# Gate, up and down projections by seven half-size products each, with activations and residual kept in DRAM

## The chip, the cores and the metric

The kernel runs on one core of a Trainium2 chip. The metric is the device time of one execution in microseconds (us). The engines are TensorE (PE in the profile), VectorE (DVE), ScalarE (ACT), GpSimd (POOL) and SyncE (SP), which issues most DMAs. Each engine works through its own instructions in a fixed order and waits on semaphores where an instruction needs another engine's or a DMA's result.

## The reference

One decoder block on x of shape (1, 1024, 1024) in float32. 16 meta tokens stand ahead of the 1024 tokens, and their outputs are dropped. The feed-forward width is 2816.

```python
def mixer(xn, w_in, conv_a_w, conv_b_w, ..., w_out):
    b_gate, c_gate, h_a, glu_val, glu_gate = jnp.split(einsum("btd,de->bte", xn, w_in), ...)
    y_a = b_gate * causal_depthwise_conv(c_gate * h_a, conv_a_w)          # 3 taps
    g = glu_val * sigmoid(glu_gate)
    y_b = silu(layer_norm(causal_depthwise_conv(g, conv_b_w) + conv_b_bias))  # 31 taps
    return einsum("bte,ed->btd", concatenate([y_a, y_b], -1), w_out)

def swiglu(xn, w_gate, w_up, w_down):
    return einsum("btf,fd->btd", silu(xn @ w_gate) * (xn @ w_up), w_down)

h = concatenate([meta_tokens, x])
h = h + rms_norm(mixer(rms_norm(h, pre_mix_norm), ...), post_mix_norm)
h = h + rms_norm(swiglu(rms_norm(h, pre_ffn_norm), ...), post_ffn_norm)
return h[:, 16:]
```

## The kernel before, in words

Every float32 product is made of three products in the fast format: an operand is split into a high part (a cast on ACT) and a low part (value minus high part, by a subtraction on DVE or GpSimd), and `mm3` (lines 87 to 90) issues high × high, high × low and low × high into one PSUM bank. A weight "unit" of 128x1024 is loaded by SP (`load_unit`, L74) and split (`split_unit`, cast L80, subtraction L81).

The stages, in the order in which PE works through them:

1. Input projection with both convolution groups, to about 270 us. The change leaves it as it is, apart from the size of the tiles that hold x.
2. Output projection in three groups of 128-token tiles, (0,1,2), (3,4,5) and (6,7) (L439 to L454): the banks are called po. `leave_psum` squares and scales what they hold, `post_mix` (L410 to L415) makes the root of the norm (`rsqrt_n`, L93 to L111, 8 or 9 operations of 128x1 on DVE) and the residual h, and `ffn_norm` (L417 to L433) normalises h (hn), transposes it on PE (pt, 8 transposes a tile) and splits it into hT. Here only tiles 0 to 3 are normalised.
3. Feed-forward, one half of the tokens (512) at a time (L458). Gate and up: for each of 22 blocks of 128 columns, 2 × 8 × 3 matmuls of 128x512 into the two banks pf (L460 to L466); then SiLU on ACT (L470) and the product on DVE (L471) leave ga, and all 22 of these tiles stay in SBUF.
4. Down, for each half of the output columns (L478): 22 blocks × 4 token tiles × 3 matmuls into four banks pd. ga is split again into gs (L492, L493). During the first of these stages `ffn_norm` of tiles 4 to 7 is run (L499 to L502). After each stage the four banks are squared (jo, L511) and scaled (L514); after the second one the root is made, the residual is added (L520 to L523) and the tile stored (L524).

So each weight of gate, up and down is loaded and split twice, once for each half of the tokens, and the residual h of all tiles stays in SBUF. The tile framework derives the order of the instructions on each engine from the program with a scheduler; tiles come from rotating pools, and an instruction that writes a tile waits until the tile's last user is done.

## Time and profile before

| | |
|---|---|
| time, median of 3 runs | 1118.02 us (1117.54 to 1118.24) |
| span of the profiled execution | 1117.3 us |
| PE, DVE, ACT, POOL busy | 1078.5, 621.2, 384.9, 217.6 us |
| first gate/up matmul | 371.05 us |
| last down matmul | 1107.25 us |
| bytes moved | 107.38 MB |

A row of the costliest groups reads: source line, engine, operation, output tile <- input tiles, shapes, number of instructions | busy time, mean ns of one | idle time of the engine just before them and what ended it. A row of the timeline begins with the start and the duration in us, and ends with the idle time before it in brackets. A row of the windows gives the stretch, its length, busy time and number of instructions (of the engine or tile chosen, otherwise of PE, PEld, DVE, ACT and POOL in this order), the granted clock, the DMA share and GB/s. PEld is the loading of a matmul's stationary operand. Matmuls overlap, so the distance between starts is their cost, not the duration.

### The profile page before, as it was taken

What the parts mean: (1) busy time and instruction counts of PE and PEld (TensorE: products, weight loads), DVE (VectorE), ACT (ScalarE), POOL (GpSimd) and SP (SyncE); (2) the same over time, 40 slices, a digit from 0 to 9 for tenths busy, and PEclk for the clock granted to TensorE, in tenths of its full rate; (3) what the DMA queues carried; (4) which work ended last, traced back from release to release, by engine and by line L of the source; (5) the groups of instructions that cost most, each with busy time, mean ns of one, the idle gap of its engine ahead of it and who ended that gap; (6) DMA issues with size and microseconds to landing.
All of it is one profiled execution on the core that took longest, in us unless ns stands there. A gap on an engine that the chain in (4) does not pass through costs nothing.

```text
span 1117.3 us, 12633 instructions
## 1 busy us (share of the span) xinstructions
PE 1078.5 (97%) x5039; PEld 909.7 (81%) x5039; DVE 621.2 (56%) x890; ACT 384.9 (34%) x508; POOL 217.6 (19%) x104
## 2 busy tenths in 40 slices
PE   8999979897998999999999999999999999999996
PEld 8999978796876888888888887888888888888885
DVE  6499999999489843322222555474333222244545
ACT  7345221236544522222222444343222222233432
POOL 3579755254555100000000000010000000000001
PEclk9999989898999999999999999999999999999999
DMA  7111111112463432223223232234222223322222
GB/s 269 57 39 57 38 38 38 39 39 94 143 234 132 132 95 94 94 95 94 94 95 96 92 95 94 94 119 145 94 95 94 95 94 97 97 92 93 97 73 75
DMA packets 30874, 107.38 MB, mean 96 GB/s; under 512 B 3424, under 2 KB 3808, under 8 KB 30816
## 3 DMA queue, kind: packets, MB, share of 16 engines
q1 hardware_dynamic: 30240, 104.94, 28.6%
q10 hardware_dynamic: 576, 1.65, 0.5%
q8 instruction: 39, 0.64, 0.2%
q14 instruction: 19, 0.16, 0.0%
HBM read 102.38 MB, written 4.19 MB: 95 GB/s over the span
## 4 chain that ended last, share of the span: by engine, by line
PE 77%; DVE 18%; ACT 1%; issue 1%; DMA 1%; SPq 0%; DVEq 0%
PE pf L89 15%; PE pf L88 15%; PE pf L90 14%; PE pd L88 7%; PE pd L90 7%; PE pd L89 7%; DVE acc L272 6%; DVE z L272 5%; PE po L89 1%; PE po L90 1%; PE po L88 1%; PE p_in_g L88 1%; PE p_in_v L88 1%; PE p_in_v L89 1%; PE p_in_g L89 1%
## 5 line engine op out<-in xcount | busy, mean ns | idle before, releaser
L521 POOL TENSOR_TENSOR raw<-raw,h 128x512 f32<-128x512 f32 x6 | 8.4, 1392 | 734.3 <-ACT raw L520 734.3
L81 DVE TENSOR_TENSOR wl_u<-ws_u,wh_u 128x1024 fp32r<-128x1024 f32 x44 | 53.9, 1225 | 164.1 <-ACT wh_u L80 164.0
L89 PE MATMUL pd<-wl_d,gs 128*128 128x512 f32 x352 | 138.9, 395 | 0.0
L90 PE MATMUL pd<-wh_d,gs 128*128 128x512 f32 x352 | 138.0, 395 | 0.0
L89 PE MATMUL pf<-hT,wh_g 128*128 128x512 f32 x352 | 138.0, 392 | 0.0
L89 PE MATMUL pf<-hT,wh_u 128*128 128x512 f32 x352 | 138.0, 392 | 0.0
L88 PE MATMUL pf<-hT,wh_g 128*128 128x512 f32 x352 | 137.9, 392 | 0.0
L88 PE MATMUL pf<-hT,wh_u 128*128 128x512 f32 x352 | 137.9, 392 | 0.0
L88 PE MATMUL pd<-wh_d,gs 128*128 128x512 f32 x352 | 137.6, 396 | 0.0
L90 PE MATMUL pf<-hT,wl_g 128*128 128x512 f32 x352 | 137.5, 391 | 0.0
L90 PE MATMUL pf<-hT,wl_u 128*128 128x512 f32 x352 | 137.5, 391 | 0.0
L471 DVE TENSOR_TENSOR ga<-pf,ga 128x512 f32<-128x512 f32 x44 | 30.4, 692 | 145.0 <-PE pf L90 145.0
L493 DVE TENSOR_TENSOR gs<-ga,gs 128x512 fp32r<-128x512 f32 x88 | 60.4, 690 | 86.8 <-ACT gs L492 76.5
L80 ACT CAST wh_u<-ws_u 128x1024 fp32r<-128x1024 f32 x44 | 46.2, 1050 | 178.6 <-PE pf L89 169.7
L272 DVE SCALAR_TENSOR_TENSOR acc<-g,pr,acc 128x512 f32<-128x512 f32 x146 | 99.8, 746 | 0.0
L80 ACT CAST wh_g<-ws_g 128x1024 fp32r<-128x1024 f32 x44 | 46.2, 1050 | 152.8 <-PE pf L89 104.4
L492 ACT CAST gs<-ga 128x512 fp32r<-128x512 f32 x88 | 54.3, 620 | 114.5 <-PE pd L89 112.4
L88 PEld LDWEIGHTS pd<-wh_d,gs 128*128 128x128 f32 x352 | 66.2, 188 | 15.9 <-ACT gs L492 0.3
L90 PEld LDWEIGHTS pd<-wh_d,gs 128*128 128x128 f32 x352 | 66.2, 188 | 15.8
L89 PEld LDWEIGHTS pd<-wl_d,gs 128*128 128x128 f32 x352 | 66.2, 188 | 15.5
L90 PEld LDWEIGHTS pf<-hT,wl_u 128*128 128x128 f32 x352 | 66.1, 188 | 14.9
L90 PEld LDWEIGHTS pf<-hT,wl_g 128*128 128x128 f32 x352 | 66.1, 188 | 15.0
(201 smaller groups left out, 2116.6 us busy)
## 6 DMA issues: line engine op xcount, KB each, us to landing
ws_g<-w_gate_u SPq DMA_DIRECT2D x44, 512.0 KB, 3.4
ws_u<-w_up_u SPq DMA_DIRECT2D x44, 512.0 KB, 3.4
ws_d<-w_down_u SPq DMA_DIRECT2D x44, 512.0 KB, 3.4
ws_o<-w_out_u SPq DMA_DIRECT2D x24, 512.0 KB, 3.4
xs<-xT SPq DMA_DIRECT2D x8, 520.0 KB, 7.3
h<-x_tok SPq DMA_DIRECT2D x8, 512.0 KB, 8.1
out<-raw SPq DMA_DIRECT2D x16, 256.0 KB, 2.0
ws_in_c<-w_in_u SPq DMA_DIRECT2D x4, 512.0 KB, 3.4
```

The costliest lines, as they stand in the source:

```text
L80: nc.scalar.copy(wh, ws)
L81: (eng or nc.gpsimd).tensor_tensor(wl, ws, wh.bitcast(F32), op=ALU.subtract)
L88: nc.tensor.matmul(o, lh, rh, start=start, stop=False)
L89: nc.tensor.matmul(o, lh, rl, start=False, stop=False)
L90: nc.tensor.matmul(o, ll, rh, start=False, stop=stop)
L272: nc.vector.scalar_tensor_tensor(o if j == CB - 1 else p, s, wb(a, j), o if j == HEAD[a] else p, op0=ALU.mult, op1=ALU.add)
L471: nc.vector.tensor_tensor(g, p[1], g, op=ALU.mult)
L492: nc.scalar.copy(s[:, 0, :], gt[f])
L493: nc.vector.tensor_tensor(s[:, 1, :], gt[f], s[:, 0, :].bitcast(F32), op=ALU.subtract)
L521: nc.gpsimd.tensor_tensor(y, y, ht[ti][:, dq], op=ALU.add)
```

## The change

One level of Strassen's scheme (Winograd's form) is put on the three matrices. A matrix is cut into 2 × 2 blocks, and seven products of half-size operands take the place of eight; sums of blocks are formed before and after.

- **Tokens.** All eight tiles are normalised before the feed-forward. The transposed tokens are kept as four raw blocks (half of the channels × half of the tokens), from which the seven token operands X are made once: B11, B21, B22 and the sums T1 to T4 (`split_big`, `halves`). `ffn_norm` writes B11 directly.
- **Gate and up.** Class `Pair` does two blocks of 128 columns at a time (11 pairs): four loads (u), the sums S1 and the in-place ones on DVE, `operand` for every product (cast on ACT, subtraction on DVE), 2 × 4 × 3 matmuls of 128x512 a product, and `leave`, which adds the banks up into pieces U2, U4, C22 and G11. Products 2 and 4 add to a bank that product 1 or 7 has filled. The products with SiLU (`glu`) and the sums of the results (`sums`) are on GpSimd. Seven combinations a pair are stored in DRAM (`store`, gd).
- **Order.** For the first two pairs: product 1 of both, 2 of both, then 6, 5, 7, 3, 4 of the first and of the second. For the others 1, 6, 2, 5, 7, 3, 4.
- **Down.** Seven passes over all 11 pairs, in the order 1, 5, 2, 6, 7, 3, 4, with four banks each (qx or qy). A pass loads its combination from DRAM (a), splits it and a block of w_down (or a difference made in place), and holds back its last two blocks; `leave1` to `leave7` add the banks up. `write` ends a tile with the residual, which was stored in DRAM (hd) by `post_mix` and is loaded back.
- **Pools.** The eight banks of the feed-forward (psf) are opened after the pools of the output projection and the transposes (pa, with aux and ps2) are closed. There are 13 pieces of 128x512 in st. Each weight is loaded once.

The diff, cut to its core:

```diff
-    def mm3(o, lh, ll, rh, rl, start, stop):
+    def mm3(o, lh, ll, rh, rl, start, stop, again=False):
...
         nc.vector.scalar_tensor_tensor(h, jk, r1, h, op0=ALU.mult, op1=ALU.add)
-        ht[i] = h
+        nc.sync.dma_start(hd[i], h)
+        return h
...
-            nc.scalar.copy(o[0], p4)
-            nc.vector.tensor_tensor(o[1], p4, o[0].bitcast(F32), op=ALU.subtract)
+            nc.scalar.copy(raw[q, i // 4][:, :, c], p4)
+            if (q, i // 4) == (0, 0):
+                nc.vector.tensor_copy(B11[0][:, :, c], p4)
+                nc.vector.tensor_tensor(B11[1][:, :, c], p4, B11[0][:, :, c].bitcast(F32), op=ALU.subtract)
...
         for i in grp:
-            post_mix(i, *left[i])
-            if i < 4:
-                if hT is None:
-                    hT = new_hT(0)
-                ffn_norm(i, hT)
+            ffn_norm(i, post_mix(i, *left[i]))
     ya.close()
+    p2.close()
+    pa.close()
+    rp = ctx.enter_context(tc.tile_pool(name="rp", bufs=5, side="right", reuse_waits="tile"))
+    st = ctx.enter_context(tc.tile_pool(name="st", bufs=13, reuse_waits="tile"))
+    psf = ctx.enter_context(tc.tile_pool(name="psf", bufs=8, space=PSUM, reuse_waits="tile"))
...
+    def operand(src, name):
+        t = wp.tile([P, 2, 512], F32R, tag=("wh", "wl")[n_ops[0] % 2], name=f"op_{name}")
+        n_ops[0] += 1
+        nc.scalar.copy(t[:, 0, :], src)
+        sub(t[:, 1, :], src, t[:, 0, :].bitcast(F32))
+        return t
...
+    X[2] = split_big(r21, "B21", (None, None))
+    halves(sub, r11, r12, r11)
+    X[5] = split_big(r11, "T1", (None, None))
+    halves(sub, r11, r22, r11)
+    X[6] = split_big(r11, "T2", (rp, rp))
+    X[3] = split_big(r22, "B22", (rp, rp))
+    halves(sub, r12, r22, r12)
+    halves(sub, r21, r21, r11)
+    X[7] = split_big(r12, "T3", (None, None))
+    X[4] = split_big(r21, "T4", (None, rp))
...
+        def a_side(self, n, m):
+            a11, a12, a21, a22 = self.w[m]
...
+            elif n == 6:
+                s1 = self.v["S1", m] = piece(f"S1{self.j}{m}")
+                add(s1, a21, a22)
+                sub(a21, a11, a21)
+                sub(a11, s1, a11)
+                s = a11
...
+            return operand(s, f"{n}_{self.j}{m}")
...
+                for k in range(4):
+                    ks = slice(k * P, (k + 1) * P)
+                    mm3(p, ops[m][:, 0, ks], ops[m][:, 1, ks], X[n][0][:, k, :], X[n][1][:, k, :], n not in (2, 4) and k == 0, k == 3, n in (2, 4))
+            for m in range(2):
+                self.leave(n, m, self.pb[where, m])
+        def leave(self, n, m, p):
+            v, j = self.v, self.j
+            if n == 1:
+                v["U2", m] = piece(f"U2{j}{m}")
+                nc.scalar.copy(v["U2", m], p)
+            elif n == 6:
+                add(v["U2", m], p, v["U2", m])
...
+                mul(v[c, 0], v[c, 0], v[c, 1], nc.gpsimd)
...
+            add(s1, g21, g22, nc.gpsimd)
+            self.store("S1", s1)
+            sub(g21, g11, g21, nc.gpsimd)
+            self.store("S3", g21)
...
+    first = [Pair(0), Pair(1)]
+    for n in (1, 2):
+        for q in first:
+            q.product(n)
+    for q in first:
+        for n in (6, 5, 7, 3, 4):
+            q.product(n)
+    for j in range(2, NP):
+        q = Pair(j)
+        for n in (1, 6, 2, 5, 7, 3, 4):
+            q.product(n)
...
+    def down(n, an, bside, banks, begin, leave):
+        late = []
+        for j in range(NP):
+            a = piece(f"a{n}_{j}")
+            nc.sync.dma_start(a, gd[an][j])
+            oa = operand(a, f"da{n}_{j}")
+            ob = operand(bside(j), f"db{n}_{j}")
...
+    def leave2(i, p):
+        squares(i, 0, p)
+        mul(D11[:, i, :], p, g0)
+    def leave6(i, p):
+        add(E1[:, i, :], p, E1[:, i, :])
+        sub(E5[:, i, :], E1[:, i, :], E5[:, i, :], nc.gpsimd)
+    def leave7(i, p):
+        t = D22[:, i, :]
+        add(t, p, E1[:, i, :])
+        squares(4 + i, 1, t)
+        mul(t, t, g1, nc.gpsimd)
...
+    down(1, "A11", lambda j: wd[j][0], QX, True, leave1)
+    down(5, "S1", in_place(sub, 0, 1, 0), QY, True, leave5)
+    down(2, "A12", lambda j: wd[j][2], QX, False, leave2)
+    down(6, "S2", in_place(sub, 0, 3, 0), QY, False, leave6)
+    down(7, "S3", in_place(sub, 1, 3, 1), QX, True, leave7)
+    down(3, "S4", lambda j: wd[j][3], QY, True, leave3)
+    down(4, "A22", in_place(sub, 2, 2, 0), QX, False, leave4)
```

What this does to the order on the engines shows at three places. The first is PE at the end of the output projection. Before, with po6 and po7 the banks of tiles 6 and 7 and pf0_00 the first bank of gate/up:

```order
L88 MATMUL po71_2901<-wh_o6_7_3030,ybh_1614 128x512
L88 MATMUL pf0_00_3113<-hT0_0_2465,wh_g0_0_3103 128x512
L89 MATMUL pf0_00_3113<-hT0_1_2466,wh_g0_0_3103 128x512
L89 MATMUL po60_2898<-wl_o6_7_3031,ybh_1614 128x512
L90 MATMUL po60_2898<-wh_o6_7_3030,ybl_1615 128x512
...
L90 MATMUL po71_2901<-wh_o6_7_3030,ybl_1615 128x512
L90 MATMUL pf0_00_3113<-hT0_0_2465,wl_g0_0_3104 128x512
```

and now, with x100 the first bank of the first pair and op_1_00 its operand:

```order
L97 MATMUL po71_2989<-wl_o6_7_3119,ybh2_1634 128x512
L98 MATMUL po71_2989<-wh_o6_7_3118,ybl2_1635 128x512
L439 MATMUL pt5_0_2974<-ident_75,hn5_2957 128x128 x4
L439 MATMUL pt5_1_2980<-ident_75,hn5_2957 128x128 x4
L439 MATMUL pt6_0_3185<-ident_75,hn6_3168 128x128 x4
L439 MATMUL pt6_1_3191<-ident_75,hn6_3168 128x128 x4
L439 MATMUL pt7_0_3232<-ident_75,hn7_3215 128x128 x4
L439 MATMUL pt7_1_3238<-ident_75,hn7_3215 128x128 x4
L96 MATMUL x100_3401<-B11h_2246,op_1_00_3395 128x512
```

The first matmuls of gate/up stood among the last of the output projection; now the transposes of tiles 5, 6 and 7 stand between the two.

The second is ACT in the middle of gate/up. Before, blocks 6 and 7:

```order
L80 CAST wh_g0_6_3493<-ws_g0_6_3491 128x1024
L80 CAST wh_u0_6_3499<-ws_u0_6_3497 128x1024
L470 ACTIVATE ga0_5_3488<-pf0_50_3438 128x512
L80 CAST wh_g0_7_3558<-ws_g0_7_3556 128x1024
L80 CAST wh_u0_7_3564<-ws_u0_7_3562 128x1024
L470 ACTIVATE ga0_6_3553<-pf0_60_3503 128x512
```

and now, at the turn from pair 3 to pair 4, where x140 and x141 are the banks of product 1 of pair 4 and op_6_40 is the first operand of its product 6:

```order
L614 ACTIVATE U230_4256<-U230_4256 128x512
L585 COPY U240_4535<-x140_4509 128x512
L585 COPY U241_4537<-x141_4522 128x512
L495 CAST op_6_40_4543<-u400_4495 128x512
L495 CAST op_2_40_4581<-u400_4495 128x512
L495 CAST op_5_40_4615<-S140_4539 128x512
L495 CAST op_6_41_4550<-u410_4499 128x512
```

The casts of the next block's weights stood ahead of what reads the banks; now the copies out of product 1's banks stand ahead of the cast for the product that PE does next.

The third is ACT in down, at a change of the banks. Before, from the first half of the output columns to the second (pd00 are the banks that close, wh_d01 and gs what the next stage needs):

```order
L80 CAST wh_d01_0_5059<-ws_d01_0_5057 128x1024
...
L80 CAST wh_d01_1_5093<-ws_d01_1_5091 128x1024
L511 ACTIVATE jo00_5041,sp00_4533<-pd000_4537 128x512
L511 ACTIVATE jo10_5044,sp01_4534<-pd001_4538 128x512
L511 ACTIVATE jo20_5047,sp02_4535<-pd002_4539 128x512
L492 CAST gs00_4532<-ga0_0_3163 128x512
```

and now, from pass 2 to pass 6 (qx are the banks that close, op_da6_0 and op_db6_0 the first operands of pass 6):

```order
L495 CAST op_db6_0_7190<-wd0_6451 128x512
L495 CAST op_db6_1_7211<-wd1_6453 128x512
L671 ACTIVATE jo00_7154,sp0_6473<-qx0_6485 128x512
L671 ACTIVATE jo10_7163,sp1_6474<-qx1_6486 128x512
L671 ACTIVATE jo20_7172,sp2_6475<-qx2_6487 128x512
L671 ACTIVATE jo30_7181,sp3_6476<-qx3_6488 128x512
L495 CAST op_db6_2_7232<-wd2_6455 128x512
L495 CAST op_da6_0_7186<-a6_0_7184 128x512
```

The next stage's first operands were cast before the squares of the old banks; now one of the two first operands is cast after all four squares.

More of the change, by code (lines that the diff above doesn't have):

```diff
@@ new lines, in write @@
+    def write(ti, parts):
+        s = sp[ti][0]
+        h = tp.tile([P, TT], F32, tag="t", name=f"hr{ti}")[:, :D]
+        nc.sync.dma_start(h, hd[ti])
+        r = rsqrt_n(s[:, 0:1], 1.0 / D, RMS_EPS, 1, f"out{ti}", s[:, 1:2])
+        for q, y in enumerate(parts):
+            dq = slice(q * 512, (q + 1) * 512)
+            if q == 1:
+                nc.scalar.activation(y, y, AF.Copy, scale=r)
+                add(y, y, h[:, dq], nc.gpsimd)
+            else:
+                nc.vector.scalar_tensor_tensor(y, y, r, h[:, dq], op0=ALU.mult, op1=ALU.add)
+            nc.sync.dma_start(out[ti * P : (ti + 1) * P, dq], y)
@@ L566 @@
         "w_up_u": units(a["w_up"][0], NF),
[L567 removed]
+        "w_down_u": a["w_down"][0].reshape(2, NP, P, D).transpose(1, 2, 0, 3),
         "par": par,
```

275 lines of the change are left out of this document (182 added, 93 removed).

## The prediction

> **What bounds the kernel now.** First the page's busy times and its chain. The columns are busy time, share of the span and instructions.
>
> ```profile
> PE 1078.5 (97%) x5039; PEld 909.7 (81%) x5039; DVE 621.2 (56%) x890; ACT 384.9 (34%) x508; POOL 217.6 (19%) x104
> ...
> PE 77%; DVE 18%; ACT 1%; issue 1%; DMA 1%; SPq 0%; DVEq 0%
> PE pf L89 15%; PE pf L88 15%; PE pf L90 14%; PE pd L88 7%; PE pd L90 7%; PE pd L89 7%; DVE acc L272 6%; DVE z L272 5%; PE po L89 1%; PE po L90 1%; PE po L88 1%; PE p_in_g L88 1%; PE p_in_v L88 1%; PE p_in_v L89 1%; PE p_in_g L89 1%
> ```
>
> TensorE (PE) is the bound: 44% of the chain is gate/up (pf), 21% down (pd). So products left out there are worth their full pace, as long as PE doesn't wait instead. I read the pace from windows that hold one stage (length, busy time and matmuls of that tile, granted clock), since a matmul's own duration (0.39) overlaps its neighbours':
>
> ```profile
> 770.00:970.00 200.00, 200.00 (x876) 1.00 0.30 95
> 990.00:1090.00 100.00, 100.00 (x431) 1.00 0.26 85
> ```
>
> 200/876 = 0.2283 us, taken as 0.2285, for gate/up, and 100/431 = 0.2320 for down.
>
> **What goes.** Gate/up has 2 × 22 × 2 × 8 × 3 = 2112 matmuls; 11 pairs × 7 products × 2 × 4 × 3 make 1848, 264 fewer: 264 × 0.2285 = 60.3 us. Down has 1056 and gets 7 × 11 × 4 × 3 = 924, 132 fewer: 30.6 us. Together 90.9 us, and 1117.3 - 90.9 = 1026.4 us if PE never waited longer than now. All else is about waits, because every helper of the scheme is put on an engine that so far idled.
>
> Can the helpers keep PE's rate? Group rows (busy time and mean ns of one, idle before), with the shapes that the new work has:
>
> ```profile
> L493 DVE TENSOR_TENSOR gs<-ga,gs 128x512 fp32r<-128x512 f32 x88 | 60.4, 690 | 86.8 <-ACT gs L492 76.5
> L81 DVE TENSOR_TENSOR wl_u<-ws_u,wh_u 128x1024 fp32r<-128x1024 f32 x44 | 53.9, 1225 | 164.1 <-ACT wh_u L80 164.0
> L492 ACT CAST gs<-ga 128x512 fp32r<-128x512 f32 x88 | 54.3, 620 | 114.5 <-PE pd L89 112.4
> L521 POOL TENSOR_TENSOR raw<-raw,h 128x512 f32<-128x512 f32 x6 | 8.4, 1392 | 734.3 <-ACT raw L520 734.3
> L414 DVE SCALAR_TENSOR_TENSOR h<-jk,s_pm,h 128x1024 f32<-128x1024 f32 x8 | 10.3, 1283 | 0.2
> L511 ACT ACTIVATE jo<-pd 128x512 f32<-128x512 f32 x16 | 9.6, 598 | 24.7 <-PE pd L90 24.6
> ...
> GB/s 269 57 39 57 38 38 38 39 39 94 143 234 132 132 95 94 94 95 94 94 95 96 92 95 94 94 119 145 94 95 94 95 94 97 97 92 93 97 73 75
> ```
>
> A steady pair is 168 matmuls, 38.4 us. It needs 33 DVE operations of 128x512 (14 low parts of operands, 8 sums of weights, 11 leaves from PSUM): 33 × 0.69 = 22.8 us. ACT has 20 × 0.62 = 12.4, GpSimd (POOL) 7 × 1.39 = 9.7. The loads (4 × 0.5 MB) and stores (7 × 0.25 MB) are 3.75 MB in 38.4 us, 98 GB/s; down reads 77 × 0.25 + 11 MB in 215 us, 141 GB/s; the slices above show 234 and 269. So no rate binds, and these operations and transfers cost nothing in steady flow. PE waits only where the order puts an operand behind something that isn't ready. I went through those places.
>
> **1. Start of the FFN: +25.6 us.** PE around the end of the output projection, before:
>
> ```profile
> 370.13 1.09 PE L88 MATMUL po<-wh_o,ybh 128*128 128x512 f32 x4
> 371.05 0.39 PE L88 MATMUL pf<-hT,wh_g 128*128 128x512 f32 x1
> ```
>
> Gate/up starts at 371.05, before the last output projection ends, on tiles 0 to 3. In the changed order the transposes of tiles 5, 6 and 7 stand ahead of the first FFN matmul, and its PSUM bank belongs to a pool that opens when the transposes' pool has closed. So two whole norm chains, one behind the other, are now on the path. Their steps, from one quiet chain of before (7 of the 8 or 9 small operations of a reciprocal root, then h):
>
> ```profile
> 361.54 0.15 DVE L103 TENSOR_SCALAR s_pm<-b_pm 128x1 int32<-128x1 int32 x1
> ...
> 363.23 1.28 DVE L414 SCALAR_TENSOR_TENSOR h<-jk,s_pm,h 128x1024 f32<-128x1024 f32 x1
> ...
> 380.04 1.06 ACT L422 ACTIVATE hn<-h 128x1024 f32<-128x1024 f32 x1 [0.55 <-DVE h L414]
> 381.01 0.18 ACT L422 ACTIVATION_READ_ACCUMULATOR hn<-h 128x1 f32 x1
> ...
> 387.56 1.28 DVE L424 SCALAR_TENSOR_TENSOR hn<-h,s_pf,gB_ffn 128x1024 f32<-128x1024 f32 x1
> ```
>
> One root is 1.7 to 2.1 us, two interleaved about 2.6. The projection ends at 371.05 + 8 × 0.232 + 0.9 (tile 4's transposes, now inside) = 373.8. Then: squares and scaled copies of tiles 6 and 7, with two operand casts and two copies between them on ACT (4 × 0.79 + 4 × 0.6, jk7 behind it): 380.2; root 2.0, h6 1.28: 383.5; square 1.5: 385.0; roots of h6 and h7 2.6, hn6 1.27, h7 1.4: 390.3; square 1.4, root 2.1, hn7 1.27: 395.1; transposes and the copy out of them 1.6: 396.7. That is 25.6 behind 371.05, ±4. The transposes of tiles 4 to 7 leave the first down stage, four times this row, of which some 0.9 doesn't overlap its neighbours: -3.6.
>
> ```profile
> 645.02 1.03 PE L429 MATMUL pt<-ident,hn 128*128 128x128 f32 x8
> ```
>
> **2. First pair's product 6: +7.** Before it stand products 1 and 2 of two pairs, 96 matmuls, 21.9 us, about 24.4 with the slow clock of point 7. DVE starts only after hn7 and has, ahead of that operand, 18 operations of 128x1024 (18 × 1.225 = 22.1) and 16 of 128x512 (11.0); neighbours overlap a little, so some 31 us, and ACT's cast, 0.6. 31.6 - 24.4 = 7, bounds 5 and 10.
>
> **3. Second pair's product 6: +7.** It follows the first pair's product 4 directly; its five sums stand behind the two leaves of that product, which wait for PE. 0.75 + 5 × 0.69 + cast 0.62 = 4.8 with DVE alone, 6.9 if GpSimd holds it up. That it can, these rows show (DVE between SBUF operands, first without and then beside GpSimd):
>
> ```profile
> 187.56 1.39 DVE L272 SCALAR_TENSOR_TENSOR z<-g,pr,acc 128x512 f32<-128x512 f32 x2
> ...
> 182.12 5.52 DVE L272 SCALAR_TENSOR_TENSOR z<-g,pr,z 128x512 f32<-128x512 f32 x2
> ...
> 181.87 5.22 POOL L366 TENSOR_TENSOR cv<-cv,u 128x1024 f32<-128x1024 f32 x2 [5.97 <-ACT u L365]
> ```
>
> DVE took 2.76 each instead of 0.70, one for each GpSimd operation of 2.61, while GpSimd kept its pace. At a pair's end GpSimd has U4's product, three sums, U2's product and the last sum queued, 6 × 1.39, so it is busy until about 4.9 us after product 4. I take the upper value, 7.
>
> **4. Nine steady pairs: +15.** Product 6 follows product 1, and on ACT both copies out of product 1's banks stand ahead of product 6's cast: 0.15 + 0.62 + 0.62 = 1.4 us after its last matmul. By DVE: 5 sums, 3 of them at GpSimd's 1.39, end 6.2 after the pair's start, cast 6.8, against 24 × 0.2285 = 5.5 for product 1: 1.4 too. Low parts that follow may be held as well, so I take 1.7 each; bounds 1.3 and 3.5, 12 to 31 us.
>
> **5. Gate/up to down: +6.** On SP the store of the last A12, which waits for GpSimd's last product, stands ahead of down's first load. Product's end 3.5 after product 4 (GpSimd's queue of point 3), two issues at 0.34, landing 2.0 (rows below) and cast 0.62 make 6.8; I take 6, since the queue may be shorter. ACT's casts of w_down are done by then. Bounds 4 and 8.
>
> ```profile
> 757.98 0.34 SPq L74 DMA_DIRECT2D ws_u<-w_up_u  x1
> ...
> out<-raw SPq DMA_DIRECT2D x16, 256.0 KB, 2.0
> ```
>
> **6. Three changes of product in down, 2 to 6, 7 to 3 and 3 to 4: +11, and the tail: +5.5.** The old banks close within 6 matmuls, 1.4 us, and on ACT four squares (0.60 + 0.19 each) and a cast stand ahead of the new operand's cast. From 1.4 before the end: 4 × 0.79 + 2 × 0.62 = 4.4 gives 3.1; where the squares read DVE's sum, 0.8 more. 3.1 + 4.0 + 4.0. The old tail is
>
> ```profile
> 1107.25 0.40 PE L90 MATMUL pd<-wh_d,gs 128*128 128x512 f32 x1
> ...
> 1112.86 1.41 DVE L523 SCALAR_TENSOR_TENSOR raw<-raw,s_out,h 128x512 f32<-128x512 f32 x2
> ```
>
> 10 us from the last matmul to 1117.3. Now four tiles come at once (4 sums, 4 products, two pairs of roots, 4 last steps on DVE): 4 × 0.7 + 4 × 0.7 + 2 × 2.6 + 4 × 0.7 + a store of 2.0: about 15.5.
>
> **7. Clock: +9.** After a wait PE ran slow (pitch 0.43 against 0.23):
>
> ```profile
> 360.23 1.17 PE L429 MATMUL pt<-ident,hn 128*128 128x128 f32 x8 [2.79 <-DVE v_pm L101]
> ...
> 362.05 0.63 PE L89 MATMUL po<-wl_o,ybh 128*128 128x512 f32 x1
> 362.48 0.63 PE L90 MATMUL po<-wh_o,ybl 128*128 128x512 f32 x1
> ...
> 360.00:372.00 12.00, 11.77 (x49) 9.65 (x50) 7.58 (x17) 7.14 (x10) 5.36 (x2) 0.86 0.40 131
> ...
> 339.41 1.06 PE L429 MATMUL pt<-ident,hn 128*128 128x128 f32 x8 [1.69 <-DVE hn L424]
> ...
> 340.55 0.39 PE L88 MATMUL po<-wh_o,ybh 128*128 128x512 f32 x1
> ```
>
> 12 us at a mean clock of 0.86 lose 1.7 us after a wait of 2.79; the wait of 1.69 was followed by no such stretch. I charge 2 us to each of points 2, 3 and 5 and 1 to each change in down, where the new product's next operands would be late anyway; the start's own is inside point 2, and point 4's waits stay under both. [...]
>
> **Sum.** -90.9 - 3.6 + 25.6 + 7 + 7 + 15 + 6 + 11 + 5.5 + 9 = -8.4. From 1117.3 that is 1108.9; the median of the runs lies 0.7 above the profiled span: 1109.6, said as 1109. The bounds of the terms (start ±4, then ±2.5, ±2, -3/+16, ±2, ±3, tail ±3, clock ±4, added as squares) are about -9 and +18.
>
> **Rivals.**
> *A. The order's waits are mostly covered.* The copies and casts run ahead, and only the start, points 2 and 3 and the tail remain: 1109 - 15 - 11 - 6 and 5 less for the clock = 1072. For it: DVE is idle 40% of a pair. Against: an engine issues in its order, and the copies do stand in front. 0.16.
> *B. Slower: GpSimd's hold on DVE decides.* Place: the end of each pair, sums and low parts of product 6. If each of the five sums and the next two low parts waits for a whole GpSimd operation, product 6 comes 0.75 + 7 × 1.39 + 0.62 - 5.5 = 5.6 late instead of 1.7, at ten pairs +39. GpSimd has 7 operations a pair, of which about half lie there, so half of it: +20, and with less clock to lose elsewhere 1129. It leads to a slower kernel from about 2.7 us a pair. For it: the rows at 182. Against: there GpSimd ran without a pause, here at 25%. 0.20. [...]
> *C. The saving is smaller than counted.* The changed matmuls share operand tiles and reopen banks; if gate/up's pace were down's 0.2320, 1848 × 0.0035 = 6.5 more; with a third of the saving gone, 30 more: 1139. That the matmuls keep their shapes and their count of loaded weights speaks against it. 0.04.
>
> **How the numbers follow.** The forecast with its own bounds has 0.60; of 1100 to 1127, 0.44 lies below 1115.8, 0.09 between 1115.8 and 1120.3, which is within 0.2% of 1118.0 and what a measurement of this kernel can't tell from no change, and 0.07 above. Faster: 0.44 + 0.16 = 0.60; same 0.09; slower: 0.07 + 0.20 + 0.04 = 0.31. With A and B down to 1075 and up to 1131, about 0.17 is left out (C, half of A, a quarter of B).
>
> **What would show it.** In the changed profile: PE's first FFN matmul near 397 (a start near 375 breaks point 1); PE waits of about 7 us before product 6 of pairs 0 and 1, behind ACT's cast; 1.3 to 2.5 before product 6 of every later pair, with the copies of U2 just ahead on ACT; 3 to 4 at three changes in down behind the squares; 15 us of tail. Pair waits above 3 us with DVE operations over 1.3 us beside GpSimd mean B, none at all mean A. A pace away from 0.2285 means C.

## The result, and the profile after

| | before | after |
|---|---|---|
| time, median of 4 runs (lowest to highest) | 1118.13 us (1117.54 to 1118.93) | 1124.43 us (1122.68 to 1125.90) |
| span of the profiled execution | 1117.3 us | 1122.2 us |
| first FFN matmul / last one | 371.05 / 1107.25 | 404.87 / 1104.19 |
| DVE, ACT, POOL busy | 621.2, 384.9, 217.6 us | 797.1, 406.6, 351.5 us |

The ratio of the times is 1.0051, 95% interval 1.0037 to 1.0065: 0.5% slower, where 0.8% faster was forecast. The time lies inside the forecast's range of 1100 to 1127, near its upper end; the direction was wrong. The first line of the page of after:

```profile
PE 1010.9 (90%) x4643; PEld 845.9 (75%) x4643; DVE 797.1 (71%) x1205; ACT 406.6 (36%) x640; POOL 351.5 (31%) x199
```

PE has 396 matmuls fewer, as computed, and its busy share fell from 97% to 90%: it now waits. The list of waits, in after (engine and tile waiting <- what ended the wait: us in total, times, longest):

```profile
PE y L96 <- ACT op L495: 22.4, 13, 6.6
```

These 13 waits are product 6 of all eleven pairs (the first two pairs wait twice each). The list of before has no wait of PE for an operand of gate/up or down. The rows of PE at which the new waits end (start, duration, and in brackets the idle time before):

```profile
378.06 0.40 PE L98 MATMUL po<-wh_o,ybl 128*128 128x512 f32 x1
...
395.95 1.94 PE L439 MATMUL pt<-ident,hn 128*128 128x128 f32 x8 [11.93 <-DVE s_pm L118]
402.24 1.94 PE L439 MATMUL pt<-ident,hn 128*128 128x128 f32 x8 [4.35 <-DVE hn L434]
404.87 0.80 PE L96 MATMUL x<-B11h,op 128*128 128x512 f32 x1 [0.70 <-ACT raw L441]
433.62 0.80 PE L96 MATMUL y<-T2h,op 128*128 128x512 f32 x1 [4.36 <-ACT op L495]
471.72 0.79 PE L96 MATMUL y<-T2h,op 128*128 128x512 f32 x1 [6.63 <-ACT op L495]
550.31 0.50 PE L96 MATMUL y<-T2h,op 128*128 128x512 f32 x1 [1.19 <-ACT op L495]
875.42 0.80 PE L96 MATMUL qx<-op_db,op_da 128*128 128x512 f32 x1 [7.20 <-ACT op_da L495]
969.91 0.50 PE L96 MATMUL qy<-op_db,op_da 128*128 128x512 f32 x1 [2.24 <-ACT op_da L495]
1033.18 0.50 PE L96 MATMUL qy<-op_db,op_da 128*128 128x512 f32 x1 [3.12 <-ACT op_da L495]
1068.14 0.79 PE L96 MATMUL qx<-op_db,op_da 128*128 128x512 f32 x1 [3.12 <-ACT op_da L495]
1084.53 0.50 PE L97 MATMUL qx<-op_db,op_da 128*128 128x512 f32 x1 [2.25 <-DVE op_db L484]
```

Read from top to bottom they are the prediction's points: the start (404.87 - 371.05 = +33.8), the first pair's product 6 (433.62), the second pair's (471.72), the steady pairs (all nine waits are 1.19), gate/up to down (875.42), the three changes in down with one late second operand (1084.53), and, behind the last matmul, the tail from 1104.19 to 1122.2. In three pieces, against the prediction's terms:

| | predicted | measured |
|---|---|---|
| start | +25.6 | +33.8 |
| first to last FFN matmul: savings, waits, clock | -90.9 - 3.6 + 7 + 7 + 15 + 6 + 11 + 9 = -39.5 | (1104.19 - 404.87) - (1107.25 - 371.05) = -36.9 |
| tail | +5.5 | +8.0 |
| sum | -8.4 | +4.9 |

So every place of waiting but one (1084.53) was found, and the sum still had the wrong sign, since all three pieces were too small: the start by 8.2, the middle by 2.6, the tail by 2.5.

The start first. It is a chain through the root of tile 5's norm, tile 5's h, ACT, and the norms of tiles 6 and 7. Its steps, the measured ends read from the rows of PE above and of DVE below:

| step of the chain | predicted | measured |
|---|---|---|
| the projection ends | 373.8 | 378.3 |
| from there to the end of the scaled copies of tiles 6 and 7 | 6.4 (380.2) | 9.7 (387.98) |
| from there to the end of tile 7's norm | 14.9 (395.1) | 14.1 (402.09) |
| from there to the first FFN matmul | 1.6 (396.7) | 2.8 (404.87) |

```profile
386.70 1.28 DVE L414 TENSOR_TENSOR jk<-po,gB_post 128x512 f32<-128x512 f32 x2
...
400.81 1.28 DVE L434 SCALAR_TENSOR_TENSOR hn<-h,s_pf,gB_ffn 128x1024 f32<-128x1024 f32 x1
```

So the roots and norms of tiles 6 and 7, which the prediction had priced from one quiet chain, took no longer than it said. What it had too short lies ahead of them and behind them. Ahead of them, DVE in after at the end of the output projection (s_pm are steps of the root on 128x1):

```profile
368.48 2.07 DVE L118 SCALAR_TENSOR_TENSOR s_pm<-t_pm,s_pm 128x1 f32<-128x1 f32 x1
...
372.11 0.14 DVE L118 SCALAR_TENSOR_TENSOR s_pm<-t_pm,s_pm 128x1 f32<-128x1 f32 x1
...
373.67 2.35 DVE L118 SCALAR_TENSOR_TENSOR s_pm<-t_pm,s_pm 128x1 f32<-128x1 f32 x1
376.06 1.29 DVE L421 SCALAR_TENSOR_TENSOR h<-jk,s_pm,h 128x1024 f32<-128x1024 f32 x1
```

and POOL there:

```profile
368.14 2.40 POOL L88 TENSOR_TENSOR wl_o<-ws_o,wh_o 128x1024 fp32r<-128x1024 f32 x1 [4.67 <-ACT wh_o L87]
373.26 2.75 POOL L88 TENSOR_TENSOR wl_o<-ws_o,wh_o 128x1024 fp32r<-128x1024 f32 x1 [2.72 <-ACT wh_o L87]
```

The same step takes 0.14 when GpSimd is idle and 2.07 or 2.35 beside a low part wl_o. Such steps had occurred in before too (the group of s_pm had a mean of 629 ns there and has 803 now), but no matmul of gate/up waited for tile 5 there. The prediction had no term for tile 5's root. By the rows the slow steps end with GpSimd's operations (370.55 and 370.54, 376.02 and 376.01), so here the hold that point 3 had read from DVE's operations of 128x512 struck an operation of one column, 2.07 against 0.14. Then ACT, in after:

```profile
377.38 1.06 ACT L432 ACTIVATE hn<-h 128x1024 f32<-128x1024 f32 x1 [3.39 <-DVE h L421]
...
379.38 2.00 ACT L503 CAST B21h<-raw 128x1024 fp32r<-128x1024 f32 x2
381.27 0.61 ACT L413 ACTIVATE sq<-po 128x512 f32<-128x512 f32 x1
...
403.72 0.62 ACT L495 CAST op<-u 128x512 fp32r<-128x512 f32 x1 [4.54 <-DMA u<-w_up_u]
404.24 1.07 ACT L441 COPY raw<-pt 128x512 f32<-128x512 f32 x2
```

The projection's last matmul started at 378.06, but the square of tile 6's bank stood behind tile 5's square (377.38, which had waited for tile 5's h), the copies of tile 4's transposes and two casts of B21, until 381.27. How much of these 3 us the two slow steps of tile 5's root make was not tried by a run. And at the end the copy that empties tile 7's transposes, for which the first FFN matmul waits, stands behind a cast that waits for a load. SP shows why that load is late:

```profile
391.08 6.46 SPq L422 DMA_DIRECT2D hd<-h  x2
...
398.07 0.78 SPq L541 DMA_DIRECT2D u<-w_up_u  x1
```

The stores of the residual h of tiles 6 and 7 wait for h, and the loads of w_up stand behind them on SP. The prediction had not priced SP's queue at this place. Next, a steady pair, on ACT in after:

```profile
549.15 0.59 ACT L585 COPY U<-x 128x512 f32<-128x512 f32 x1 [2.17 <-PE x L98]
549.63 1.14 ACT L495 CAST op<-u 128x512 fp32r<-128x512 f32 x2
```

Product 1's last bank closes at 549.1, the copy of it goes first, then the cast for product 6, and PE goes on at 550.31: the picture of point 4. Last, the tail. GpSimd's last additions of the residual:

```profile
1116.17 2.97 POOL L481 TENSOR_TENSOR D<-D,hr 128x512 f32<-128x512 f32 x2 [1.96 <-ACT D L681]
```

They take 1.5 each, the last two start only from 1116.17 on, and the last stores are issued from 1117.95 on. The prediction's tail had "4 last steps on DVE" and left out the other four, which are on GpSimd: two from 1111.27 on, and these two.

### The profile page after: what moved, and what is told of

It reads as the page before. It is cut to its first block, busy times and chain, and to the rows that moved or that the text cites. A ratio compares the mean times of both kernels' runs of the same rounds, so it can differ in the third digit from the quotient of the medians.

```text
span 1122.2 us, 12694 instructions
## 1 busy us (share of the span) xinstructions
PE 1010.9 (90%) x4643; PEld 845.9 (75%) x4643; DVE 797.1 (71%) x1205; ACT 406.6 (36%) x640; POOL 351.5 (31%) x199
## 5 line engine op out<-in xcount | busy, mean ns | idle before, releaser
L495 ACT CAST op<-u 128x512 fp32r<-128x512 f32 x132 | 79.7, 620 | 161.1 <-PE y L98 102.1
L484 DVE TENSOR_TENSOR op_da<-a,op_da 128x512 fp32r<-128x512 f32 x77 | 59.9, 782 | 61.2 <-ACT op_da L495 60.6
L484 DVE TENSOR_TENSOR op<-u,op 128x512 fp32r<-128x512 f32 x132 | 89.0, 688 | 10.7 <-ACT op L495 10.6
L495 ACT CAST op_da<-a 128x512 fp32r<-128x512 f32 x77 | 47.3, 622 | 107.4 <-PE qx L98 49.0
L88 POOL TENSOR_TENSOR wl_o<-ws_o,wh_o 128x1024 fp32r<-128x1024 f32 x24 | 59.4, 2485 | 72.1 <-ACT wh_o L87 72.1
L97 PE MATMUL qx<-op_db,op_da 128*128 128x512 f32 x176 | 71.1, 404 | 2.5 <-DVE op_db L484 2.5
L98 PE MATMUL qx<-op_db,op_da 128*128 128x512 f32 x176 | 68.0, 398 | 0.0
L484 DVE TENSOR_TENSOR op_db<-wd,op_db 128x512 fp32r<-128x512 f32 x77 | 55.8, 724 | 9.9 <-ACT op_db L495 9.9
L96 PE MATMUL qx<-op_db,op_da 128*128 128x512 f32 x176 | 52.5, 404 | 10.3 <-ACT op_da L495 10.3
L280 DVE SCALAR_TENSOR_TENSOR z<-g,pr,z 128x512 f32<-128x512 f32 x48 | 61.4, 1301 | 0.0
L495 ACT CAST op_db<-wd 128x512 fp32r<-128x512 f32 x77 | 47.6, 618 | 13.0 <-PE qx L98 7.4
L97 PE MATMUL qy<-op_db,op_da 128*128 128x512 f32 x132 | 52.1, 395 | 0.0
L98 PE MATMUL qy<-op_db,op_da 128*128 128x512 f32 x132 | 49.9, 393 | 0.0
L96 PEld LDWEIGHTS qx<-op_db,op_da 128*128 128x128 f32 x176 | 34.5, 196 | 18.5 <-ACT op_da L495 11.2
```

Of the source, the lines that this page charges most:

```text
L88: (eng or nc.gpsimd).tensor_tensor(wl, ws, wh.bitcast(F32), op=ALU.subtract)
L96: nc.tensor.matmul(o, lh, rh, start=start, stop=False, skip_group_check=again)
L97: nc.tensor.matmul(o, lh, rl, start=False, stop=False, skip_group_check=again)
L98: nc.tensor.matmul(o, ll, rh, start=False, stop=stop, skip_group_check=again)
L280: nc.vector.scalar_tensor_tensor(o if j == CB - 1 else p, s, wb(a, j), o if j == HEAD[a] else p, op0=ALU.mult, op1=ALU.add)
L484: (eng or nc.vector).tensor_tensor(o, a, b, op=ALU.subtract)
```

## The experiments

The theory was that of the prediction: the waits come from the order in which ACT, DVE and SP do the helpers, so another order takes them away with the same work. The rivals: GpSimd holds DVE up (B), or the matmuls are slower (C). Each ratio is against before, on the same chip. Before's own median was 1118.13 to 1118.98 in these comparisons, so a difference of two medians of this table is good to about 1 us.

| kernel | median us | ratio to before (95%) |
|---|---|---|
| changed kernel | 1124.43 | 1.0051 (1.0037 to 1.0065) |
| e1, banks without the pool's barrier | 1116.78 | 0.9981 (0.9971 to 0.9991) |
| e2, operands two products ahead | 1095.55 | 0.9785 (0.9769 to 0.9802) |
| e3, next pass's operands ahead of the squares | 1111.31 | 0.9927 (0.9912 to 0.9942) |
| e4, without GpSimd in gate/up | 1106.34 | 0.9880 (0.9865 to 0.9895) |
| e5, norm chains interleaved | 1117.38 | 0.9986 (0.9976 to 0.9995) |
| e6, e2 + e3 + e5 | 1082.47 | 0.9681 (0.9667 to 0.9696) |
| e7, e6 + e1 and more | 1076.69 | 0.9627 (0.9611 to 0.9643) |
| e8, a slot for the second pair's sums | 1112.27 | 0.9941 (0.9924 to 0.9957) |
| e9, B11 split later | 1122.73 | 1.0028 (1.0018 to 1.0037) |

**e1: is the start only the pool's barrier?** The banks come from the older pools, so that the first FFN matmuls need not wait for the transposes' pool to close, and the first two pairs' loads get tiles that are free early.

```diff
-    psf = ctx.enter_context(tc.tile_pool(name="psf", bufs=8, space=PSUM, reuse_waits="tile"))
...
-        return psf.tile([P, 512], F32, tag="p", name=name)
+        if name[:2] in ("y1", "qa"):
+            return aux.tile([P, 512], F32, tag="a", name=name)
+        return ps2.tile([P, 512], F32, tag="p", name=name)
...
-                    if (m + i) % 2:
+                    if (i or (j, m) == (1, 1)) if j < 2 else (m + i) % 2:
```

> The feed-forward's banks come from the pools of the output projection and of the transposes, and the first two pairs' weights lie so that product 1 has its loads early; nothing else is changed. 36 matmuls of product 1 (two and a half of the four halves of it) then stand ahead of the last transposes. Theory (the start is one path: norm chains of tiles 5 to 7, then DVE's 31 us of token operands, then product 6 of the first pair, which begins at 433.6 now): the first feed-forward matmul comes at about 379 instead of 404.9, but product 6 comes at most 5 us earlier, and the time is 1117 to 1122. Rival (product 1's own wait of 34 us is the cost): 1124.4 - 25 = about 1099.

PE in e1:

```profile
376.92 0.48 PE L96 MATMUL x<-B11h,op 128*128 128x512 f32 x1
...
403.93 1.94 PE L439 MATMUL pt<-ident,hn 128*128 128x128 f32 x8 [4.35 <-DVE hn L434]
428.37 0.79 PE L96 MATMUL y<-T2h,op 128*128 128x512 f32 x1 [6.75 <-ACT op L495]
```

The first FFN matmul moved 28 us ahead (376.92), but tile 7's transposes still stand at 403.93 (402.24 in after), and product 6 of the first pair at 428.37 is only 5.2 earlier than in after (at most 5 was expected). What binds it is the norm chain and the token operands behind it on DVE; the barrier and the loads hide in that path, and both together are worth 7.7 us by the medians, not 28.

**e2: operands ahead.** The operands of each product are made two products ahead in the program, ahead of the leaves of the products between, and one load of each odd pair gets its tile from another pool, to be there in time; the work is the same.

```diff
+        while ready < min(i + 3, len(seq)):
+            jr, nr = seq[ready]
+            if jr not in pairs:
+                pairs[jr] = Pair(jr)
+            pairs[jr].prep(nr)
+            ready += 1
+        pairs[j].product(n)
...
-                    if (m + i) % 2:
+                    if (m + i) % 2 or (j % 2 and m):
```

> The operands of gate/up are made two products ahead of their use in the program, so that the sums S1 stand ahead of the leaves of products 3 and 4 on DVE and the casts for product 6 ahead of the copies of U2 on ACT; one load of each odd pair is put into another pool, so that all four are there in time. Theory (order on ACT and DVE makes the wait of 1.19 us, 1.36 with the pitch, before product 6 of nine pairs, and 6.6 before that of the second pair): these waits go and so does 2.3 of slow clock: 12.2 + 6.8 + 2.3 = 21 less, 1103, and not below 1100. Rival (DVE, held by GpSimd, has no time to give): the waits come back in front of other products and the time stays above 1115.

The nine waits of 1.19 and the 6.63 are gone, the first pair's 4.36 is 1.00. The first matmul of product 1 of two pairs in a row, in after:

```profile
543.35 0.40 PE L96 MATMUL x<-B11h,op 128*128 128x512 f32 x1
...
583.94 0.40 PE L96 MATMUL x<-B11h,op 128*128 128x512 f32 x1
```

and in e2:

```profile
566.14 0.40 PE L96 MATMUL x<-B11h,op 128*128 128x512 f32 x1
...
605.22 0.40 PE L96 MATMUL x<-B11h,op 128*128 128x512 f32 x1
```

A pair takes 40.59 in after and 39.08 in e2: the wait of 1.19 costs 1.51 a pair (predicted 1.7), 13.6 for nine. The gain by the medians is 1124.4 - 1095.6 = 28.8, some 7 more than expected. The nine waits (13.6), the first pair's (4.7 - 1.0 = 3.7), the second pair's (7.0) and the slow clock behind these two (3.1 and 2.8, as read under point 7 below) make 30.2; the expectation had nothing for the first pair. Against that the start is 0.7 later in e2 (405.54). Its steady pairs, without waits, also give the pace (length, busy time and matmuls, granted clock, DMA share, GB/s):

```profile
500.00:840.00 340.00, 339.81 (x1462) 1.00 0.35 128
```

340/1462 = 0.2326 us a matmul at full clock, where the prediction had 0.2285 from before. Over 1848 matmuls that is 7.6 us: rival C's first figure (6.5) came true beside the forecast. Before itself had two paces in gate/up; its first stage, by the same columns, ran at 200/870 = 0.2299:

```profile
400.00:600.00 200.00, 200.00 (x870) 1.00 0.30 95
```

Against the mean of both stages, 0.2291, the loss is 6.5 us. In down it goes the other way, in after:

```profile
880.00:960.00 80.00, 80.00 (x354) 1.00 0.39 111
```

80/354 = 0.2260, against 0.2320 in before: 924 × 0.006 = 5.5 us less. Why the pace differs at the same shapes and a full clock was not found.

**e3: down.** The first operands of the next pass are made ahead of the squares of this pass's banks.

```diff
-            oa = operand(a, f"da{n}_{j}")
-            ob = operand(bside(j), f"db{n}_{j}")
+            oa, ob = pre if j == 0 and pre else down_ops(n, an, bside, j)
...
+        nxt = down_ops(*then, 0) if then else None
```

> In down, the first operands of a pass are loaded and cast before the old banks are squared; nothing else is changed. Theory: the waits of 2.2, 3.1 and 3.1 us at three changes of pass go, with 2.7 of slow clock: about 11 less, 1113. Rival (the next operands are then late instead, since the two held-back blocks keep two of three buffers): 1118 or more.

The waits of 2.24, 3.12, 3.12 and 2.25 (with a small one of 0.27) became 0, 1.28 + 0.60, 1.28 + 0.81 and 0, and the slow stretches of down behind them went too (the matmuls behind 1030.30 and 1062.76, where the waits of 1.28 end in e3, start 0.22 to 0.24 apart from the second on; behind 1068.14 in after it was 0.43); the medians give 13 us. So the order in which a pass's first operands are made was the cause of the wait of 2.24 and of a part of the two of 3.12, with the clock behind them. The rest of those two stays: a cast of w_down there starts only when PE has released a buffer (1029.11), as the rival said, at a smaller price. The wait of 2.25 was of another kind. In after DVE makes the low parts ahead of it in 1.79 and 1.75 us (1081.02 and 1082.73) beside GpSimd's last additions for tiles 0 to 3, against 0.68 without; in e3 one of the two falls beside them, and PE doesn't wait.

**e4: GpSimd.** All of GpSimd's work in gate/up is left out: the products of the two halves of SwiGLU and the sums of the results; the other engines keep theirs.

```diff
-            else:
-                mul(v[c, 0], v[c, 0], v[c, 1], nc.gpsimd)
...
-            add(s1, g21, g22, nc.gpsimd)
-            self.store("S1", s1)
-            sub(g21, g11, g21, nc.gpsimd)
+            self.store("S1", g21)
```

> Leaves out all of GpSimd's work in gate/up (the second half of SiLU's products and the four sums of each pair; what is stored are unsummed pieces), with the order of the other engines kept. Theory (the copies on ACT alone keep product 6 as late as DVE does): the wait of 1.19 before product 6 of a pair stays within 0.2, that of the second pair falls from 6.6 to about 4.8, and the one before down from 7.2 to about 4: 1118 to 1120. Rival B (GpSimd's hold on DVE makes the pairs' wait): the wait falls below 0.5 at nine pairs, and the time to 1110 or less.

The group of DVE's sums at a pair's start, in after:

```profile
L481 DVE TENSOR_TENSOR S<-u 128x512 f32<-128x512 f32 x22 | 25.0, 1180 | 0.0
```

in e4:

```profile
L481 DVE TENSOR_TENSOR S<-u 128x512 f32<-128x512 f32 x22 | 14.1, 683 | 0.0
```

and PE at a steady pair of e4:

```profile
541.03 0.50 PE L96 MATMUL y<-T2h,op 128*128 128x512 f32 x1 [1.19 <-ACT op L495]
```

GpSimd does hold DVE: its sums take 1180 ns beside it and 683 without. But the nine waits stay at exactly 1.19, because the cast stands behind the copy out of product 1's bank whatever DVE does. Rival B is refuted for the steady pairs. The kernel was 12 us faster than expected all the same, since two other waits fell further than expected: the second pair's 6.63 vanished, and the one ahead of down went from 7.20 to 1.86; with the clock behind them that is some 17 of the 18 us. The second follows point 5: in after SP's store of A12 (871.51) waits for GpSimd's last product and the first load for down stands behind it. The first was new, and e8 took it up.

**e5: the norm chains.** The roots of tiles 6 and 7 are interleaved, with four small tiles instead of two and a high priority.

```diff
-    sm = ctx.enter_context(tc.tile_pool(name="sm", bufs=2))
+    sm = ctx.enter_context(tc.tile_pool(name="sm", bufs=4))
...
-        left = {i: leave_psum(i, pm[i]) for i in grp}
-        for i in grp:
-            ffn_norm(i, post_mix(i, *left[i]))
+        with tc.high_priority(offset=4000) if grp[0] == 6 else ExitStack():
+            left = {i: leave_psum(i, pm[i]) for i in grp}
+            hh = {i: post_mix(i, *left[i]) for i in grp} if grp[0] == 6 else {}
+            for i in grp:
+                ffn_norm(i, hh[i] if i in hh else post_mix(i, *left[i]))
```

> The norm chains of tiles 6 and 7 are interleaved: four instead of two buffers for the small tiles of the roots, and both residuals ahead of both norms in the program. All else as in the changed kernel. Theory (two serial chains on DVE and ACT make the start late, and the first pair's product 6 follows them by DVE's work): the last transposes come about 5 us earlier than 402.2, product 6 of the first pair by as much, and the four roots at the end are made at once, 1 to 2 us less: 1117 to 1119. Rival (the start is set by something else, such as the loads of the first pair's weights, one of which landed at 403.7): the transposes come earlier, but the first feed-forward matmul by less than 2 us, and the time stays above 1122.

The first FFN matmul starts at 400.17 (4.7 earlier), the first pair's product 6 waits 2.10 + 1.01, and the time is 7 us lower. The order of these steps is worth that; with both residuals ahead, their stores and the loads behind them on SP go earlier too (a load of w_up is issued at 392.89, in after at 398.07). The tail stayed at 18.5 us (1095.17 to 1113.7) although the small tiles for all four roots are there, so these were not what made it long; GpSimd's four additions then stand in a row (1103.79 to 1110.62).

**e6 and e7: together.** e6 is e2 + e3 + e5. e7 adds e1, makes B22, T3 and T4 after the first pair's operands, loads down's first combination ahead of the last stores, and puts the last tile's second half on DVE.

```diff
+        if i == 4:
+            with tc.high_priority(offset=-60):
+                rest()
...
+    pre = down_ops(1, "A11", lambda j: wd[j][0], 0)
+    pairs[NP - 1].product(4)
```

> The three changes together that were tried one by one: operands of gate/up two products ahead, the first operands of a pass of down ahead of the squares, and the interleaved chains. Theory (the waits are at different places and add up): 1124.4 - 28 - 12 - 6 = 1078. Rival (they share a cause, for example DVE's or ACT's time, so that a wait taken away here comes back there): above 1090.

> As the one with three changes, and further: the feed-forward's banks from the older pools so that product 1 starts early; the operands B22, T3 and T4 made after those of the first pair's product 6 where DVE is free; the first load of down ahead of the last stores of gate/up on SP; the last tile's second half ended by DVE instead of GpSimd. Theory: product 6 of the first pair comes some 5 us earlier, the wait before down falls from 7 to 2 with its slow clock of 1.7, and the end takes 1 to 2 us less: 1078 - 13 = 1065. Rival (the early products only fill a time that DVE needs anyway, and the last sums of gate/up are late for pass 5 instead): 1075 or more.

The gains of e2, e3 and e5 add up to 29 + 13 + 7 = 49, and e6 is 42 us below the changed kernel, 4 to 5 short of the expected 1078: most of them are independent, not all. e7 is another 6 lower, 3.7% faster than before, but at 1077 and not at the expected 1065; its rival had said 1075 or more. Its first pair's product 6 still waits, behind the same chain, so the early products 1 and 2 mostly fill time that the chain needs anyway.

```profile
396.74 1.94 PE L439 MATMUL pt<-ident,hn 128*128 128x128 f32 x8 [8.52 <-DVE hn L434]
424.00 0.79 PE L96 MATMUL y<-T2h,op 128*128 128x512 f32 x1 [8.38 <-ACT op L497]
```

In both, PE, DVE, ACT and GpSimd have the same number of instructions as in after, to within one. The seven products are worth having with an order that feeds them.

**e8: a slot.** The second pair's two sums S1 lie in a free tile of tp instead of in two of the 13 pieces; GpSimd keeps all its work.

```diff
-                s1 = self.v["S1", m] = piece(f"S1{self.j}{m}")
+                if self.j == 1:
+                    self.s1t = getattr(self, "s1t", None) or tp.tile([P, TT], F32, tag="t", name="s1t")
+                    s1 = self.v["S1", m] = self.s1t[:, m * 512 : (m + 1) * 512]
...
```

> The changed kernel, and the two sums S1 of the second pair lie in a free 128x1040 tile of tp instead of in two of the 13 pieces; all of GpSimd's work and the program's order stay. Slot theory: the 6.6 us wait before the second pair's product 6 comes from S1 waiting for a piece that GpSimd and a store must free; with a slot of its own the sum goes ahead of the first pair's leaves on DVE, and that wait falls to 1.2 or less and its 2.3 us of slow clock go: 1124 - 6.6 + 1.2 - 2 = 1116 to 1118. Rival, GpSimd's hold on DVE itself: the wait stays at 5 or more and the time within 2 us of 1124. The nine waits of 1.19 stay in both.

DVE around these sums, in after:

```profile
465.13 0.69 DVE L481 TENSOR_TENSOR U<-x,U 128x512 f32<-128x512 f32 x1 [2.13 <-PE x L98]
465.73 2.35 DVE L481 TENSOR_TENSOR S<-u 128x512 f32<-128x512 f32 x2
468.01 2.35 DVE L484 TENSOR_TENSOR u<-u,u 128x512 f32<-128x512 f32 x2
```

and in e8:

```profile
406.44 0.69 DVE L481 TENSOR_TENSOR s1t<-u 128x512 f32<-128x512 f32 x1
...
445.95 0.69 DVE L481 TENSOR_TENSOR s1t<-u 128x512 f32<-128x512 f32 x1
```

In after both sums stand behind the last leaf of the first pair, at 465.73; with a slot of their own they ran at 406.44 and 445.95, and the wait of 6.63 is gone. Down begins 10.2 us earlier (865.21), and the time fell by 12, more than the 6 to 8 expected; the rest, 2 us, is inside down, where the wait of 2.25 for a low part was 1.42 in this run. So the place of these sums, and with it the second pair's wait, comes from the pool of pieces: GpSimd does the same work in e8. Once they stand there, GpSimd's grip lengthens the wait: four sums take 1.18 each in after, and 0.64 each in e4 (455.04 to 457.5). That e4 removed the wait by needing three pieces fewer a pair fits its earlier sums, but was not tried apart.

**e9: B11.** B11 is split after the transposes of all tiles, not on DVE in each of tiles 0 to 3.

```diff
-                nc.vector.tensor_copy(B11[0][:, :, c], p4)
-                nc.vector.tensor_tensor(B11[1][:, :, c], p4, B11[0][:, :, c].bitcast(F32), op=ALU.subtract)
...
+    for h in range(2):
+        k = slice(2 * h, 2 * h + 2)
+        nc.scalar.copy(B11[0][:, k, :], raw[0, 0][:, k, :])
+        nc.vector.tensor_tensor(B11[1][:, k, :], raw[0, 0][:, k, :], B11[0][:, k, :].bitcast(F32), op=ALU.subtract)
```

> The changed kernel, with B11 split by two casts and two subtractions of 128x1024 after the eight tiles' transposes instead of from PSUM in each of tiles 0 to 3 on DVE. Theory: those 8 DVE operations beside GpSimd's low parts are what delayed the end of the output projection by 4.5 us against before; PE's waits in it fall from 9.3 to 5.3 or 6 us and its last matmul ends near 374.5. The start of gate/up then depends on whether the split is hidden in the norm chains of tiles 6 and 7 (first FFN matmul near 401) or comes behind them (near 405): 1119 to 1124. Rival, the waits come from the norm chains of tiles 4 and 5 in front of the transposes alone: waits stay above 8 and the last matmul of the projection at 378.

PE in e9:

```profile
375.96 0.39 PE L98 MATMUL po<-wh_o,ybl 128*128 128x512 f32 x1
...
404.72 0.80 PE L96 MATMUL x<-B11h,op 128*128 128x512 f32 x1 [1.44 <-ACT raw L441]
```

A split result. The projection ends 2.1 us earlier than in after, so B11 accounts for about half of the 4.5 by which it was late, and not for all of it as the theory had it; the other half was not tried apart. And the start didn't move (404.72 against 404.87): the norm chain came 0.9 earlier, but the copy of tile 7's transposes still stood behind the cast that waits for w_up (403.56 in e9). ACT's first square of tile 6 in e9:

```profile
380.36 0.60 ACT L413 ACTIVATE sq<-po 128x512 f32<-128x512 f32 x1
```

It is only 0.9 earlier than in after (381.27), again straight behind the casts of B21 and 4.2 behind the end of the projection. So when the projection ends is not what sets the start; by the rows it is what stands ahead of the squares on ACT, and at the end SP's queue.

## Why the prediction was wrong

**Savings.** The counts were right. The pace was not: 0.2326 in gate/up instead of 0.2285 (+7.6), 0.2260 in down instead of 0.2320 (-5.5). That the two nearly cancel was luck. "If gate/up's pace were down's" was held for unlikely because the shapes stay the same; that was no proof.

**Point 1, the start, is the step that failed:** +33.8 instead of +25.6, twice the bound of 4. "The projection ends at ... 373.8" was 378.3, and the chain from there took 26.6 instead of 22.9. Of the 4.5 by which the projection was late, e9 puts about half on B11's split, and the other half stays open. Of the 3.7 in the chain, 3.3 lie in the squares and copies, where the sum let ACT begin when the projection ends: tile 5's square, tile 4's copies and the casts of B21 stood ahead until 381.27. Another 1.2 lie at the end, where tile 7's transposes ran at a granted clock of 0.50 (1.94 instead of the 1.03 of the row at 645.02) and the last copy stood behind a cast that waited for a load behind the residual's stores. The sum had priced none of these. The roots and norms between were 0.8 shorter than priced. About 1.9 us of the start were charged wrongly in the other direction: eight matmuls of the projection that before came after 371.05 only moved.

**Points 2 and 3.** 4.36 + 0.34 and 6.63 + 0.34 against 7 and 7. The first wait is shorter because the start before it is later: its end was put at 396.7 + 24.4 + 7 = 428.1 and came at 433.6, and in e1, where PE starts 28 us earlier, it still came at 428.4, so DVE's chain sets it. Point 3 has the right size, and its working came true as far as it went: five sums behind the last leaf, four of them lengthened by GpSimd (1.18 each, 0.64 in e4). What it took as given, that the sums must stand there, came from a missing piece (e8).

**Point 4.** Nine waits of 1.19, 1.51 with the new start: 13.6 against 15, for the reason given (e2, e4).

**Points 5 and 6.** 7.2 against 6; 11.0 in down against 11, which was luck in part: 8.5 are the three changes, by e3 only in part for the reason given, and 2.5 a late low part of w_down in the middle of a pass (2.25 and 0.27), which was not foreseen.

**Tail.** +8.0 against +5.5. GpSimd's four additions were left out of the sum; but e7, which has the last of them on DVE, has a tail of 18 us as well (1056.73 to 1074.9), so what would shorten it is open.

**Point 7, the clock.** Behind the waits of 1.19 and 2.24 the granted clock stayed at 1.00 for the next 3 us. Behind the longer ones it was 0.50 for a while: its mean over the 10 us from 404.87, 433.62, 471.72 and 875.42 was 0.79, 0.69, 0.72 and 0.76, and over the 5 us from 1033.18, 1068.14 and 1084.53 it was 0.66, 0.68 and 0.66. That loses 2.1 us behind the start, 3.1 and 2.8 behind the first two pairs' product 6, 2.4 at the entry to down, and 1.7, 1.6 and 1.7 in down: some 15 together, against 9. 2.1 of it belong to the start's own, which the prediction had put inside point 2.

A wait's length alone doesn't decide it: 2.24 us at 969.91 cost no clock, and 2.25 at 1084.53 did. In the trace of after the stretches of 0.50 last 3.41 us or 2, 3 or 8 times that (the one that the kernel's end cuts off aside), and all begin and end on one grid of that step. Two steps of the grid around each of the two waits (length, busy time of PE and matmuls, granted clock, DMA share, GB/s):

```profile
965.52:968.94 3.42, 2.15 (x10) 1.00 0.22 39
968.94:972.35 3.41, 2.44 (x11) 1.00 0.74 269
...
1081.57:1084.98 3.41, 1.16 (x6) 1.00 0.99 326
1084.98:1088.39 3.41, 3.41 (x10) 0.50 0.92 317
```

The wait of 2.24 is shared by two steps, which are idle for 1.27 and 0.97 (3.42 - 2.15 and 3.41 - 2.44); the wait of 2.25 lies whole in one, and the step behind that one has 0.50. In the traces of before and after, leaving out the step in which the kernel starts, each of the 17 steps at full clock in which PE was idle for 2.08 us or more was followed by one at 0.50, and none with 1.74 or less was; between the two there was no step.

**Rivals.** A, that the waits are covered, did not happen, but e2, e3 and e6 show that they can be by order alone. B is refuted where it was placed; GpSimd's hold on DVE did show in point 3 and in the wait of 2.25 in down. C happened in part. The sign was lost because three errors of 2.5 to 8 us fell on one side of a forecast of -8.

## What to carry to other kernels

When a scheme removes work from the bounding engine, list every place where that engine's next operand stands behind something else, and price the first chain with everything that stands ahead of its steps in each engine's queue, and with every DMA ahead of its loads. Then move the operand ahead: two products ahead here was worth 29 us of 1124, with the same work. Where an operation comes later in its engine's order than its inputs would allow, look at the slots of its pool: one free tile was worth 12 us here.

## What the runs showed of the hardware

- A step of 128x1 on DVE took 2.07 and 2.35 us beside GpSimd's 128x1024 subtraction, 0.14 without. A sum of 128x512 took 1.18 us beside GpSimd's work on 128x512 and 0.68 without.
- Matmuls of the same shape at a granted clock of 1.00 ran at 0.2299, 0.2283 and 0.2320 us in three stages of before, 0.2326 in gate/up of e2 and 0.2260 in down of after. What sets it is open.
- In before and after the granted clock fell to 0.50 in steps of 3.41 us, each time behind a step in which PE had been idle for 2.08 us or more (17 times; no step with 1.74 or less was followed by one at 0.50). A wait of 2.24 us (969.91), shared by two steps that were idle for 1.27 and 0.97, was followed by 3 us at 1.00; one of 2.25 us (1084.53), whole in one step, by 5 us at 0.66, some 1.7 us lost.
